# The first load of a streaming kernel as two transfers, of the even and of the odd partitions

## Chip, cores and metric

The kernel runs on one core of a Trainium2 chip. The metric is the device time of one execution in microseconds (us).

## The reference

```python
x = float32[32, 512, 2048]
x1, x2 = x[..., :1024], x[..., 1024:]
out = x1 * (1 / (1 + exp(-x1))) * x2          # silu(x1) * x2, float32[32, 512, 1024]
```

The kernel must read 134.2 MB and write 67.1 MB, and there is little arithmetic.

## The kernel before

The 16384 rows are taken in 16 tiles. In a tile each of the 128 partitions holds 8 whole rows (64 KB in, 32 KB out). Two input and two output buffers rotate. ScalarE issues the loads and does the silu, VectorE multiplies, and SyncE issues the stores. The first load is moved by hand ahead of the barrier that all engines pass at the start.

```python
def issue_ahead_of_the_first_barrier(nc):
    head, body = nc.main_func.blocks[:2]
    load = next(ins for ins in body.instructions if type(ins).__name__ == "InstDMACopy")
    ...                                     # cut: puts `load` before ScalarE's barrier drain

def load(i):
    xt = in_pool.tile([P, K, in_cols], dt, name="xt")              # K = 8, in_cols = 2048
    nc.scalar.dma_start(out=xt[:, :plan[i][1], :], in_=view(x_flat, i))
    loaded[i] = xt

load(0)
load(1)
for i in range(n_tiles):                                           # 16 tiles
    ...                                     # cut
    for c in range(0, k, KC):                                      # four chunks of two rows
        ...                                 # cut: silu into ot on ScalarE, then ot *= x2 on VectorE
        if last:
            nc.sync.dma_start(out=ov[:, c:ce, :], in_=ot[:, c:ce, :])
    if not last:
        nc.sync.dma_start(out=ov, in_=ot[:, :k, :])
    if i + 2 < n_tiles:
        load(i + 2)
```

Of the kernel before, what the change touches and what calls it, by code (L numbers as in the profile page):

```python
# [1 line left out]

# [4 lines left out]


def issue_ahead_of_the_first_barrier(nc):




    head, body = nc.main_func.blocks[:2]
    load = next(ins for ins in body.instructions if type(ins).__name__ == "InstDMACopy")
    at = next(
        j for j, ins in enumerate(head.instructions)
        if ins.engine == load.engine and type(ins).__name__ == "InstDrain"
    )
    body.instructions = [ins for ins in body.instructions if ins.name != load.name]  # L20
    head.instructions = head.instructions[:at] + [load] + head.instructions[at:]


@with_exitstack
def kernel(
    ctx: ExitStack,
    tc: tile.TileContext,
    x: bass.AP,
    out: bass.AP,
):  # L30






    nc = tc.nc
    P = nc.NUM_PARTITIONS

    x_flat = x.flatten_outer_dims()  # L40
    out_flat = out.flatten_outer_dims()
    num_rows, in_cols = x_flat.shape
    half = in_cols // 2
    dt = x_flat.dtype

    K = 8
    KC = 2
    PLAN = [K] * (num_rows // (P * K))

    in_pool = ctx.enter_context(tc.tile_pool(name="in_pool", bufs=2))  # L50
    out_pool = ctx.enter_context(tc.tile_pool(name="out_pool", bufs=2))

    plan = []
    row = 0
    for k in PLAN:
        plan.append((row, k))
        row += P * k
    assert row == num_rows
    n_tiles = len(plan)

    def view(flat, i):
        row0, k = plan[i]
        return flat[row0:row0 + P * k].rearrange("(p k) d -> p k d", k=k)

    nc.at_finalize(issue_ahead_of_the_first_barrier)


    ctx.enter_context(tc.manual_schedule())

    loaded = {}  # L70

    def load(i):
        xt = in_pool.tile([P, K, in_cols], dt, name="xt")
        nc.scalar.dma_start(out=xt[:, :plan[i][1], :], in_=view(x_flat, i))
        loaded[i] = xt

    load(0)
    load(1)
    for i in range(n_tiles):
        k = plan[i][1]  # L80
        xt = loaded.pop(i)
        last = i == n_tiles - 1
        ov = view(out_flat, i)
        ot = out_pool.tile([P, K, half], dt, name="ot")
        for c in range(0, k, KC):
            ce = min(c + KC, k)
            nc.scalar.activation(  # L87
                out=ot[:, c:ce, :],
                in_=xt[:, c:ce, :half],
                func=mybir.ActivationFunctionType.Silu,  # L90
            )
            nc.vector.tensor_mul(  # L92
                out=ot[:, c:ce, :],
                in0=ot[:, c:ce, :],
                in1=xt[:, c:ce, half:],
            )
            if last:
                nc.sync.dma_start(out=ov[:, c:ce, :], in_=ot[:, c:ce, :])
        if not last:
            nc.sync.dma_start(out=ov, in_=ot[:, :k, :])  # L100
        if i + 2 < n_tiles:
            load(i + 2)


# [1 line left out]
_INS = ['x']  # L106
_OUTS = [((32, 512, 1024), 'float32')]


# [23 lines left out]
```

## Time and profile before

| | before |
|---|---|
| time, median of 3 runs | 470.96 us (470.91 to 471.08) |
| span of the profiled run | 468.9 us |
| share of the 16 DMA engines' span that packets take | 66.4% loads + 33.2% stores |
| VectorE, ScalarE busy | 30%, 25% |

From the page of the kernel before: the DMA engines' busy tenths in 40 slices, the two queues (packets, MB, share of sixteen engines' span), the shares of the chain that ended last, and the activation table load (busy us, mean ns, idle time before it and what ended that).

```profile
span 468.9 us, 269 instructions
...
DMA  9899999999999998999999999999999989999998
...
q10 hardware_dynamic: 2304, 134.22, 66.4%
q1 hardware_dynamic: 2736, 67.11, 33.2%
...
DMA 80%; DVE 15%; ACT 3%; DVEq 0%; issue 0%
...
L87 ACT ACT_TABLE_LOAD x1 | 1.3, 1283 | 1.3 <-PEq L117 1.3
```

The two queue shares add to 99.6%: there is almost no moment at which a DMA engine has nothing to move. The chain alone would mislead here. It names loads, multiply and silu, because those steps hand the buffers round; but while the chain is in the multiply, the DMA still works on what was issued earlier (DMA share 0.95 and 412 GB/s from 46.48 to 55.39 us, the chain's first multiply).

The timeline of the kernel before, from its start to the first store (start us, duration us, engine, line, what; "x2" on an issue row merges two issues):

```profile
start us, us, engine line op out<-in xcount [idle before <-releaser]
0.13 1.13 ACTq L74 DMA_DIRECT2D xt<-in_x_dram  x2
...
1.29 1.28 ACT L87 ACT_TABLE_LOAD   x1 [1.29 <-PEq L117]
21.88 7.31 ACT L87 ACTIVATE ot<-xt 128x2048 f32<-128x2048 f32 x4 [19.31 <-DMA xt<-in_x_dram]
23.82 8.90 DVE L92 TENSOR_TENSOR ot<-ot,xt 128x2048 f32<-128x2048 f32 x4 [23.82 <-ACT ot L87]
32.74 0.38 SPq L100 DMA_DIRECT2D out_dram<-ot  x1
32.75 0.35 ACTq L74 DMA_DIRECT2D xt<-in_x_dram  x1
```

The first load is issued at 0.13 us and has landed at 21.88 us. The table that silu needs is loaded early, at 1.29 us, and costs nothing. The first store is issued at 32.74 us. The trace's single packet records add that the first packet starts at 1.14 us and that a 64 KB load packet takes 2.42 us on its engine.

### The profile page before, as it was taken

Reading aid. Unit: us, or ns where it says so; the run is one execution under the profiler, and the core shown is the slowest. Engines: PE = TensorE matmul, PEld = TensorE weight load, DVE = VectorE, ACT = ScalarE, POOL = GpSimd, SP = SyncE. Lnnn points to the kernel's source line nnn. Section 1 sums busy time; section 2 is a strip of 40 time slices with the busy share of each in tenths; the row PEclk is TensorE's granted clock in tenths of the full one; section 3 lists DMA queues with packets and bytes.
Section 4 is the critical chain, followed back from the end, with each engine's and each line's share of the span. In section 5 each row is a group of like instructions: output and inputs, shape, how many; then the busy total and the mean of one; then the engine's idle time right before and its main releaser. Section 6 shows DMA issues by size and latency. Waiting matters only on the chain.

```text
span 468.9 us, 269 instructions
## 1 busy us (share of the span) xinstructions
DVE 142.3 (30%) x64; ACT 118.2 (25%) x65; POOL 0.2 (0%) x4
## 2 busy tenths in 40 slices
DVE  0070705106061160601507025070250702407034
ACT  1142406023060330603206032060420604106051
POOL 0000000000000000000000000000000000000000
DMA  9899999999999998999999999999999989999998
GB/s 431 375 447 403 447 447 447 403 419 431 447 447 403 447 492 363 442 492 391 458 403 439 456 447 403 409 442 447 447 403 444 467 386 447 442 419 481 400 409 354
DMA packets 5042, 201.35 MB, mean 429 GB/s; under 512 B 560, under 2 KB 560, under 8 KB 560
## 3 DMA queue, kind: packets, MB, share of 16 engines
q10 hardware_dynamic: 2304, 134.22, 66.4%
q1 hardware_dynamic: 2736, 67.11, 33.2%
q14 instruction: 2, 0.02, 0.0%
HBM read 134.22 MB, written 67.11 MB: 429 GB/s over the span
## 4 chain that ended last, share of the span: by engine, by line
DMA 80%; DVE 15%; ACT 3%; DVEq 0%; issue 0%
DMA xt<-in_x_dram 80%; DVE ot L92 15%; ACT ot L87 3%; DVEq L128 0%
## 5 line engine op out<-in xcount | busy, mean ns | idle before, releaser
L92 DVE TENSOR_TENSOR ot<-ot,xt 128x2048 f32<-128x2048 f32 x64 | 142.3, 2286 | 319.5 <-ACT ot L87 319.5
L87 ACT ACTIVATE ot<-xt 128x2048 f32<-128x2048 f32 x64 | 116.9, 1897 | 338.8 <-DMA xt<-in_x_dram 338.8
L87 ACT ACT_TABLE_LOAD x1 | 1.3, 1283 | 1.3 <-PEq L117 1.3
L117 POOL MEMSET const-uint8-127<- 128x1 uint8 x1 | 0.1, 102 | 0.0
L117 POOL MEMSET const-bfloat16-1.0<- 128x1 bf16 x1 | 0.1, 101 | 0.0
L117 POOL MEMSET const-float32-0.0<- 128x1 f32 x1 | 0.1, 98 | 0.2 <-issue 0.2
L117 POOL MEMSET const-float32-1.0<- 128x1 f32 x1 | 0.1, 98 | 0.0
## 6 DMA issues: line engine op xcount, KB each, us to landing
out_dram<-ot SPq DMA_DIRECT2D x15, 4096.0 KB, 39.8
out_dram<-ot SPq DMA_DIRECT2D x4, 1024.0 KB, 5.7
xt<-in_x_dram ACTq DMA_DIRECT2D x16, 47.1
```

The lines of the kernel that those rows point to most:

```text
L87: nc.scalar.activation(out=ot[:, c:ce, :], in_=xt[:, c:ce, :half], func=mybir.ActivationFunctionType.Silu,)
L92: nc.vector.tensor_mul(out=ot[:, c:ce, :], in0=ot[:, c:ce, :], in1=xt[:, c:ce, half:],)
L117: nc = _bacc.Bacc("TRN2", target_bir_lowering=False, num_devices=1)
```

## The change

The intent is an earlier start: a first transfer of 64 partitions has half the packets (64 instead of 128; the trace has 2048 of 64 KB for 16 loads), so they might flow sooner. Both transfers stand ahead of the barrier. The split is by even and odd partitions, not by halves.

```diff
-def issue_ahead_of_the_first_barrier(nc):
+def issue_ahead_of_the_first_barrier(nc, count):
...                                   # cut: moves the first `count` loads instead of one
+    STARTING = [slice(0, None, 2), slice(1, None, 2)]
...
+    def load_parts(queue, dst, src, split):
+        for ps in STARTING if split else [slice(None)]:
+            queue.dma_start(out=dst[ps], in_=src[ps])
...
-        nc.scalar.dma_start(out=xt[:, :plan[i][1], :], in_=view(x_flat, i))
+        load_parts(nc.scalar, xt, view(x_flat, i), split=i == 0)
...
-            nc.sync.dma_start(out=ov, in_=ot[:, :k, :])
+            nc.sync.dma_start(out=ov, in_=ot)
```

The last line is the same access (k is always K).

More of the change, by code (lines that the diff above doesn't have):

```diff
@@ L6 @@
 from concourse._compat import with_exitstack
-def issue_ahead_of_the_first_barrier(nc):
+def issue_ahead_of_the_first_barrier(nc, count):
     head, body = nc.main_func.blocks[:2]
-    load = next(ins for ins in body.instructions if type(ins).__name__ == "InstDMACopy")
+    loads = [ins for ins in body.instructions if type(ins).__name__ == "InstDMACopy"][:count]
     at = next(
         j for j, ins in enumerate(head.instructions)
-        if ins.engine == load.engine and type(ins).__name__ == "InstDrain"
+        if ins.engine == loads[0].engine and type(ins).__name__ == "InstDrain"
     )
-    body.instructions = [ins for ins in body.instructions if ins.name != load.name]
-    head.instructions = head.instructions[:at] + [load] + head.instructions[at:]
+    names = {ins.name for ins in loads}
+    body.instructions = [ins for ins in body.instructions if ins.name not in names]
+    head.instructions = head.instructions[:at] + loads + head.instructions[at:]
 @with_exitstack
@@ L63, in view @@
         return flat[row0:row0 + P * k].rearrange("(p k) d -> p k d", k=k)
-    nc.at_finalize(issue_ahead_of_the_first_barrier)
+    nc.at_finalize(lambda nc: issue_ahead_of_the_first_barrier(nc, len(STARTING)))
     ctx.enter_context(tc.manual_schedule())
+    def load_parts(queue, dst, src, split):
+        for ps in STARTING if split else [slice(None)]:
+            queue.dma_start(out=dst[ps], in_=src[ps])
     loaded = {}
```

## The prediction

> **What bounds the kernel now.** The DMA engines. The page's DMA row reads 8 or 9 of 10 in all slices, at a mean of 429 GB/s; the two queues' packets take 66.4% + 33.2% = 99.6% of sixteen engines' span. VectorE is busy 30%, ScalarE 25%. The packets in the trace agree: from the first (1.14 us) to the last (467.63 us) about sixteen are in flight. A 64 KB load packet takes 2418 ns, a 32 KB store packet 1213 ns, an 8 KB one 309 ns; 2048, 1920 and 512 of them are 464.9 us on sixteen engines; the measured sum is 466.8 us. Most of the rest lies in two places: the first sixteen packets (about 3.0 instead of 2.42 us) and the sixteen before the first store (about 3.3 us). The chain of waits (80% loads, 15% multiply, 3% silu) is the loop that hands buffers back; the DMA never runs dry waiting for it.
>
> **What the change does.** (1) Load 0 (8.39 MB) becomes two transfers of 64 partitions each on one queue. Packet sizes and bytes stay: 4 + 4 instead of 8 packets per engine. (2) One more issue of about 0.35 us stands before ScalarE's barrier, so load 1 is issued at about 1.3 instead of 0.92 us, behind some 19 us of load 0: no cost. (3) The first tile waits for two semaphores. The instruction listing puts the second wait on the activation table load, so that load (1.28 us) moves from the idle time at 1.3 us to after the landing of tile 0. First silu, first store and load 2 come some 1.3 us later (store about 34.0 instead of 32.7 us). Load 1 still moves until past 40 us, so the DMA does not run dry: off the path. (4) The possible gain: the first packet starts 1.0 us after its issue. [...] first packets start an estimated 0 to 0.25 us earlier (half of the 0.38 us issue at most). Only this is on the critical path. (5) The full-tile store's slice is the same access.
>
> **Predicted time: 470.8 us, range 469.9 to 472.2.** Faster by over 2%: 1%; within 2%: 87%; slower by over 2%: 12%.
>
> **What would show it.** First packet at 0.9 to 1.15 us; landing of load 0 at 21.5 to 22.0 us; table load at about 21.8 us, first silu at about 23.1; DMA share and mean GB/s unchanged; last packet within 0.5 us of 467.6.
>
> **What would make it wrong.** [...] no trace here shows 64 strided ones. [...] load 0 runs at about half rate, packets near 4.8 us, landing near 41 us, an estimated +19 us (8 packets x 2.42 us): about 490 us. [...] Lesser risk: the later first store shifts the mixing of loads and stores; at most about 1 us.

The forecast comes to the 470.96 us before less about 0.2 us for the earlier start of step (4): 470.8. The condition of that gain, that the first packets of 64 rows come sooner than those of 128, was a supposition; the traced 0.38 us issue, of which half is 0.19, is all that the estimate has. Under "What would make it wrong" is an estimate: 4.8 us, 41 us and +19 us are what half of the traced rate (2.42 us per packet) comes to. It is no part of the 470.8 and lies outside the range, in the 12% for "slower by over 2%".

## More of the kernel before

All runs quoted here are at a granted clock of 1.0. Kernels sent together ran on one chip, beside the kernel before.

## The result, and the profile after

Ratios are computed as the mean time of one kernel's fast runs over that of the other's of the same rounds, so they are not quite the ratios of the medians.

| | before | after |
|---|---|---|
| time, median of 6 runs | 471.02 us (470.71 to 471.44) | 471.51 us (471.30 to 472.15) |
| ratio, 95% interval | | 1.0014 (1.0001 to 1.0027) |
| span of the profiled run | 468.9 us | 470.3 us |

The change is within 2%, and a little slower. The profiled run of the changed kernel took 472.13 us, near the top of its six, so its trace shows more than the typical loss.

The same lines of the page, of the changed kernel:

```profile
span 470.3 us, 272 instructions
...
DMA  9999999999999999999999999999999999999997
...
q10 hardware_dynamic: 2320, 134.22, 66.3%
q1 hardware_dynamic: 2736, 67.11, 33.1%
...
DMA 80%; DVE 15%; ACT 3%; DVEq 0%; issue 0%
...
L95 ACT ACT_TABLE_LOAD x1 | 1.3, 1283 | 22.4 <-DMA xt<-in_x_dram 22.4
```

Bytes, shares and chain are the same. The 16 new packets on the load queue are of 4 bytes: 272 with 17 transfers, 256 with 16. The trace has sixteen of them at 11.60 to 12.28 us, where the engines' fourth load packets end (11.60 to 12.29 us). One line differs: the table load now waits 22.4 us, for a load.

The timeline of the changed kernel:

```profile
0.13 2.20 ACTq L76 DMA_DIRECT2D xt<-in_x_dram  x3
...
22.36 1.28 ACT L95 ACT_TABLE_LOAD   x1 [22.36 <-DMA xt<-in_x_dram]
23.66 7.31 ACT L95 ACTIVATE ot<-xt 128x2048 f32<-128x2048 f32 x4
25.60 8.90 DVE L100 TENSOR_TENSOR ot<-ot,xt 128x2048 f32<-128x2048 f32 x4 [25.60 <-ACT ot L95]
34.52 0.38 SPq L108 DMA_DIRECT2D out_dram<-ot  x1
```

ScalarE sees the landing at 22.36 instead of 21.88 us (the last packet of load 0 ends 0.44 us later), the table load comes after it, and the first store is 1.78 us later. None of these lines says which of them costs time. For that the packets must be read.

**How the packets were read.** A record gives queue, start, duration and size, but not the engine. Each packet was therefore given to the engine whose previous packet ended at its start, which is a reconstruction: a second working of it, with other tolerances, moves single latenesses by up to 0.15 us. Three things were worked out for each run: the start of the first packet; when the engines' first store packets start (the earliest and the median of the first sixteen); and how late the slowest of the 16 engines is by 60 us (the end of its first packet, less 2.42 us, plus what its later load packets took beyond 2.42 us).

| | first packet | last engine ends its first packet | first store issued | first store packets, earliest / median | slowest engine late by | span |
|---|---|---|---|---|---|---|
| before | 1.14 | 4.60 | 32.74 | 38.9 / 39.1 | 3.04 | 468.87 |
| after | 1.45 | 5.04 | 34.52 | 39.2 / 42.2 | 4.89 | 470.35 |

Two things stand out. The first packet is 0.31 us later, not earlier: the first issue took 541 to 542 ns in two runs, against 376 ns before. That is 0.17 of the 0.31 us; the rest passes between the end of the issue and the first packet (0.78 instead of 0.64 us). And in the changed kernel the engines no longer begin to store together: two of them start 2.4 us or more ahead of the other 14 (39.2 and 39.7 against 42.1 to 42.7 us).

Followed to the end, these two are also the last to finish, at 468.87 and 469.03 us; the other 14 finish by 468.31. All 16 engines have 280 data packets in this reconstruction, and from 60 us on their load packets take the usual 2.42 us, so what is lost early stays lost. The last packet ends 1.41 us later than before. Of that, 0.30 is the later start and 0.06 the first packets, both as means over the 16 engines; 0.59 is the mean growth of the stalls at the first stores, and 0.46 is how much further the last engine lies behind the mean.

### The profile page after: what moved, and what is told of

It is laid out like the page before. It is cut to its first block, busy times and chain, and to the rows that moved or that the text cites. A ratio compares the mean times of both kernels' runs of the same rounds, so it can differ in the third digit from the quotient of the medians.

```text
span 470.3 us, 272 instructions
## 1 busy us (share of the span) xinstructions
DVE 142.4 (30%) x64; ACT 118.2 (25%) x65; POOL 0.2 (0%) x4
## 4 chain that ended last, share of the span: by engine, by line
DMA 80%; DVE 15%; ACT 3%; DVEq 0%; issue 0%
DMA xt<-in_x_dram 80%; DVE ot L100 15%; ACT ot L95 3%; DVEq L136 0%
## 5 line engine op out<-in xcount | busy, mean ns | idle before, releaser
L95 ACT ACT_TABLE_LOAD x1 | 1.3, 1283 | 22.4 <-DMA xt<-in_x_dram 22.4
```

Of the source, the lines that this page charges most:

```text
L95: nc.scalar.activation(out=ot[:, c:ce, :], in_=xt[:, c:ce, :half], func=mybir.ActivationFunctionType.Silu,)
```

## The experiments

Medians are of the kernel's own 4 to 6 runs against the kernel before on the same chip. In the edits, the lines that allocate `warm_pool` and `warm` are cut where they add nothing, and function names are shortened (`Silu` for `mybir.ActivationFunctionType.Silu`).

**The changed kernel again.** No edit.

> The changed kernel once more, to see how firm its +0.14% is. Start theory (the two 64-row issues bring the first packet 0.3 us later, and everything follows): first packet at 1.4 to 1.5 us, time +0.3 us (ratio 1.0006). Table theory (activation table load behind the landing makes the first store 1.3 us later, which lengthens the stall ahead of the first store): time +0.4 to +0.6 us, with the stalled packets ahead of the first store again over 3.4 us. Noise theory: ratio within 1.000 +- 0.0005.

Measured: 471.54 us against 470.90 (ratio 1.0016, interval 1.0003 to 1.0029). First packet at 1.45 us; one engine starts to store at 39.7 us, the median at 42.1. The loss came again, both intervals exclude 1, and noise is an unlikely cause. The trace of this run, the slowest of its five, shows one thing that the first does not: near the end the DMA engines run partly dry (last columns: DMA share, GB/s).

```profile
457.00:457.50 0.50, 0.50 (x2) 0.50 (x1) 0.00 (x0) 1.00 0.30 131
457.50:458.00 0.50, 0.50 (x1) 0.50 (x1) 0.00 (x0) 1.00 0.16 66
```

In the reconstruction twelve engines are idle there for 0.2 to 0.8 us: the first of them is done with the older store at 457.62 us, and the store of the last tile's first chunk, issued at 457.33, starts its first packet at 458.16. (In the first trace it is issued at 456.61, and nothing runs dry.) The end is still set by one engine, at 469.78 us; the other 15 finish by 468.35.

**Split, with the table loaded early.**

```diff
     load(0)
     load(1)
+    warm = warm_pool.tile([P, 2], dt, name="warm")
+    nc.vector.memset(warm[:, :1], 0.0)
+    nc.scalar.activation(out=warm[:, 1:], in_=warm[:, :1], func=Silu)
```

> The changed kernel with a one-column silu ahead, so that the table load is back at the start. First silu about 22.35 us instead of 23.66, first store about 33.2. Start theory: still +0.3 us against before, as the changed kernel. Table theory: back to before within 0.1 us, stall ahead of the first store about 0.8 us in each engine.

Measured: 471.37 us against 470.90 (1.0013, 1.0000 to 1.0025). First silu at 22.59 us, first store at 33.46. The time did not return to that of before, so an early table alone does not cure the loss. That the rest stays with the start is not shown: in this trace all engines begin to store within 0.9 us, and yet one ends at 469.12 us, 1.0 us after the other 15, for a reason that was not found. The stall ahead of the first store was about 1.05 us per engine, more than the 0.8 that the table theory asked for.

**One load, with a late table.**

```diff
     load(0)
     load(1)
+    nc.scalar.activation(out=warm, in_=loaded[0][:, 0, :1], func=Exp)   # meant to bring a second table load
```

> The kernel before, with a one-column exponential that waits for load 0 ahead of the first silu, so that the silu table is loaded only after the landing (about 1.3 to 1.6 us more until the first store, near 34.3). Start theory: time as before within 0.1 us. Table theory: +0.3 to +0.5 us, stall ahead of the first store over 1 us in each engine.

Measured: 471.79 us against 470.90 (1.0019, 1.0006 to 1.0031), with the first packet at 1.15 us and the first store at 34.41, 1.67 us later (one table load took 1.28 us in the kernels before and after). So +0.9 us with an unchanged start: the start cannot be all. This looks like the table theory, but the delay of the store and the table load itself are not yet told apart.

**One load, behind the barrier.**

```diff
-    nc.at_finalize(issue_ahead_of_the_first_barrier)
```

> The kernel before with load 0 issued after the barrier: a measure of what a later first packet is worth. First issue at about 0.6 to 0.9 us instead of 0.13, so the first packet 0.5 to 0.75 us later. Start theory: the time grows by that much (+0.5 to +0.75 us, ratio about 1.0013), one for one. If the start is not what counts: within 0.2 us of before.

Measured: 471.82 us against 470.90 (1.0017, 1.0003 to 1.0030); first packet at 1.75 us, 0.61 later. The time grew by 0.9 us, more than the 0.5 to 0.75 expected; the interval reaches from 0.1 to 1.4 us, so it agrees with a late start that is paid in full, and does not fix the rate.

**The kernel before, against itself.** No edit.

> The kernel before, against itself: how far two sets of runs of one program lie apart, and a second trace of it. Ratio 1.000 within 0.0005; first packet at 1.14 us; stall ahead of the first store again about 0.87 us per engine (sixteen packets of about 3.3 us).

Measured: 470.98 us against 471.17 (0.9996, 0.9983 to 1.0009), first packet at 1.15 us, sixteen stalled packets, slowest engine 3.17 us late. Two sets of runs of one program differ by 0.2 us in the median. Single executions stray further: one of the 11 of the kernel before took 472.5 us, and one of the six with the 2.4 us delay 472.64.

**One load, first tile delayed by scratch work: 0.8, 2.4 and 4.0 us.** The three differ in the columns only:

```diff
     load(0)
     load(1)
+    nc.scalar.activation(out=warm[:, :850], in_=loaded[0][:, 0, :850], func=Silu)
...                             # the other two: two such lines, of 2048 and 300, of 2048 and 1900 columns
```

> The kernel before, with one extra silu of 850 columns into a scratch tile ahead of the first tile: first store about 0.8 us later (33.5 us), table load and first packet unchanged. Start theory: time as before. Later-is-worse theory (a later first store costs in proportion): about +0.4 us. Phase theory (what counts is where the first store falls in the 2.42 us that one load packet takes): between 0 and +0.6 us.

> The same with about 2.3 to 2.5 us of scratch silu: the first store one whole load packet later (about 35.2 us). Start theory: as before. Later-is-worse theory: +1.0 us or more, as the 1.67 us delay of the late table cost +0.9. Phase theory: back to before within 0.2 us, stall ahead of the first store about 0.87 us per engine.

> The same with about 3.9 us of scratch silu: first store near 36.7 us, one load packet after that of the late-table run (34.4). Start theory: as before. Later-is-worse theory: +2 us. Phase theory: about +0.9 us as the late-table run, with engines that switch to stores one packet apart.

Measured, first store at 33.72, 35.19 and 36.44 us: 470.83, 471.09 and 471.10 us against 471.17 (0.9992, 0.9999, 0.9994; all intervals hold 1). A first store up to 3.7 us later costs nothing that these times can see, and "later is worse" falls. (The traces of the two longer delays are 0.3 and 0.4 us longer than that of the kernel before, again, which the times don't resolve.) The phase theory, as it was put, missed too: it expected +0.9 us at the longest delay. That run came out at 36.44 us rather than one whole packet after the late-table run (which would be 36.83), so it did not test the intended phase. In the two longer delays the engines still begin to store together, within 0.8 us. In the shortest they do not: 13 begin at 39.0 to 39.6 us and three at 41.9 to 42.1. No engine there loses more than 1.4 us to stalls, and the last packet ends at 467.71 us, as before (467.62). So engines out of step need not be costly.

This led to the straggler theory, a reading of these traces that the next runs test. The end of the program is set by the slowest of 16 equally loaded DMA engines (280 data packets each; in the changed kernel the two that were ahead end last, at 468.87 and 469.03 us). If one or two engines take their first store packet a packet ahead of the others, they stall twice where the others stall once, and nothing afterwards lets them catch up.

**One load, delayed by 1.5 us**, to the moment of the late-table run, with no second table load (the same edit with 1670 columns).

> The kernel before, with about 1.5 us of scratch silu ahead of the first tile, so that the first store is issued near 34.4 us, as in the late-table run, but with no second table load. Straggler theory (when the first store is issued about 0.5 to 1.2 us after the engines' last packet starts, one or two engines pick it up a packet ahead of the rest and stall twice; the slowest engine sets the end): first store packets spread over more than 2 us, the slowest engine over 4.3 us late by 60 us, time +0.5 to +0.9 us. Table theory (the table load itself costs): as before, within 0.2 us, as the delays of 1.0, 2.5 and 3.7 us were.

Measured: 471.68 us against 470.93 (1.0012, 1.0000 to 1.0025). The timeline shows the first store at 34.31 us:

```profile
21.95 1.60 ACT L81 ACTIVATE warm<-xt 128x1670 f32<-128x1670 f32 x1 [19.37 <-DMA xt<-in_x_dram]
...
34.31 0.37 SPq L103 DMA_DIRECT2D out_dram<-ot  x1
```

The earliest store packet starts at 39.2 us, the median at 41.9, and the slowest engine is 4.95 us late. Three engines of the reconstruction, from 35.6 us on (L is a load packet, S a store packet; start + duration in us):

```
this run, an ordinary engine   L 35.64+2.42 | L 38.05+3.90 | S 41.95+1.21 | S 43.16+1.21 | L 44.37+2.42
this run, the engine ahead     L 35.89+3.34 | S 39.22+1.21 | L 40.43+4.36 | S 44.79+1.21 | S 46.01+1.21
kernel before, one engine      L 35.71+3.24 | S 38.95+1.21 | L 40.16+2.42 | S 42.58+1.21 | S 43.79+1.21
```

The engine ahead loses 0.92 us at its first stall, as all engines do in the kernel before (0.8 to 1.0 us). Then it loses another 1.94 us while the rest stall; the ordinary engine loses 1.48 us once. In the four runs with one or two engines ahead, these engines lose 2.3 to 2.9 us in all, and no other engine more than 1.7. In the late-table run, too, the engine ahead ends last, at 468.86 us, with the other 15 done by 467.86. The delays of 0.98, 2.45 and 3.70 us cost nothing that shows in the times, and this one between them does, so neither lateness nor the table load is needed for the loss. Two of the five executions took 471.1 us, as the kernel before; the profiled one is the slowest, so an engine ahead is shown for that one only.

**Split, delayed by 1.1 us more**, so that the first store meets the engines at the point of their packets where the kernel before meets them (the same edit with 1190 columns, on the changed kernel).

> The changed kernel with 1.1 us of scratch silu more, so that its first store (near 35.65 us) falls 1.6 to 2.3 us after the engines' packet starts, as in the kernel before. Straggler theory: first store packets within 1 us of each other, the slowest engine 3.5 to 4.0 us late, time +0.3 to +0.45 us against before, which is faster than the changed kernel's +0.65. Later-is-worse: slower than the changed kernel.

Measured: 471.20 us (471.18 to 471.42) against 470.93 (1.0006, 0.9993 to 1.0018). It does more work on the first tile than the changed kernel, stores later (35.67 us), and is closer to the kernel before. First store packets are at 41.7 / 42.1 us, and the slowest engine is 3.96 us late. The remaining +0.27 us is about the 0.31 us by which its first packet is late, though its own interval holds 1. The interval overlaps that of the changed kernel, which ran on another chip, so the times alone do not prove the step; the trace shows no engine ahead.

**Split by halves.**

```diff
-    STARTING = [slice(0, None, 2), slice(1, None, 2)]
+    STARTING = [slice(0, 64), slice(64, 128)]
```

> The changed kernel, split at partition 64 instead of by even and odd. [...] load 0 packets near 4.8 us, landing near 41 us, time about +19 us (490 us). If the engines' own rate is all that limits: as the changed kernel. The first issue's duration tells whether the 541 ns come from the 64 rows (again about 541) or from the step of two (about 375).

Measured: 491.31 us against 470.93 (1.0431, 1.0416 to 1.0445). Bandwidth while only loads run (last columns: DMA share, GB/s), first of the changed kernel, then of the halves:

```profile
core 0: us, DVE busy (x) ACT busy (x) POOL busy (x), PEclk, DMA share, GB/s
5.00:20.00 15.00, 0.00 (x0) 0.00 (x0) 0.00 (x0) 1.00 1.00 433
```

```profile
5.00:20.00 15.00, 0.00 (x0) 0.00 (x0) 0.00 (x0) 1.00 1.02 210
```

All 16 engines are busy in both (shares 1.00 and 1.02), but in the halves each packet takes 5.12 us instead of 2.42. The runs don't show why; they show that 64 partitions in a row ran at about half the rate (210 GB/s), and 64 in steps of two did not (433). The clause cut from the expectation gave a ground that no trace shows; what is left of that estimate is again half of the traced rate. The first issue took 548 ns, as for the even partitions (541), so its length comes with the 64-row transfer, not with the step of two.

**Two transfers of all 128 partitions**, each with half of every partition's rows.

```diff
-    STARTING = [slice(0, None, 2), slice(1, None, 2)]
+    STARTING = [slice(0, K // 2), slice(K // 2, K)]
...
-            queue.dma_start(out=dst[ps], in_=src[ps])
+            queue.dma_start(out=dst[:, ps], in_=src[:, ps])
```

> Load 0 in two transfers ahead of the barrier, but of all 128 partitions, each with half of every partition's rows (32 KB a packet). If it is the 64-row transfer that starts late: first issue about 375 ns, first packet at 1.14 us as before; if it is two issues in a row, near 1.45 us. The first tile's work begins after half the load (first silu near 12 us), first store near 28.5 us. Time within 0.3 us of before if no engine is split from the rest; +0.5 to +0.9 if one is.

Measured: 471.97 us against 470.93 (1.0022, 1.0009 to 1.0036). The first issue took 376 ns and the first packet starts at 1.14 us, as before: two issues in a row did not delay the start here, 64-row transfers did (first issue 541 to 548 ns; first packet at 1.45 us in the changed kernel). No engine is ahead of the others (34.2 / 34.3 us). The expectation of a time within 0.3 us failed, and for another reason. Two windows near the end, of this run:

```profile
455.00:457.00 2.00, 1.56 (x1) 2.00 (x2) 0.00 (x0) 1.00 0.91 393
457.00:458.50 1.50, 1.50 (x2) 1.50 (x2) 0.00 (x0) 1.00 0.01 0
```

and of the kernel before:

```profile
455.00:457.00 2.00, 2.00 (x2) 2.00 (x2) 0.00 (x0) 1.00 0.68 295
457.00:458.50 1.50, 1.50 (x2) 1.34 (x1) 0.00 (x0) 1.00 0.96 404
```

Windows count a packet where it starts, so single shares are rough, but 0.01 means that no data packet starts for 1.5 us; from the packets' ends each DMA engine is idle for 0.7 to 1.6 us. The earlier first store (28.38 us) shifted the turns of loads and stores. The last load landed at 453.5 instead of 451.0 us, and the store before the last tile's had drained in 15 of 16 engines by 457.6 us, before the last tile's first chunk was ready (issued at 457.76). In the kernel before that chunk is issued at 455.29 us and the first engine is done with the older store at 457.0, a margin of 1.7 us. In the two traces of the changed kernel this margin is 1.2 and 0.3 us; in the second the engines ran partly dry, as said above.

**The runs together** (us; "late" is the slowest engine at 60 us; the last two experiments, with other packets or idle engines, are left out):

| run | first packet | first store packets, earliest / median | late | span | span − late | median minus before |
|---|---|---|---|---|---|---|
| before, again | 1.15 | 39.0 / 39.2 | 3.17 | 468.95 | 465.8 | −0.2 |
| delay 2.4 | 1.15 | 41.6 / 41.9 | 3.71 | 469.27 | 465.6 | −0.1 |
| delay 4.0 | 1.14 | 41.9 / 42.0 | 3.69 | 469.38 | 465.7 | −0.1 |
| split, delay 1.1 | 1.45 | 41.7 / 42.1 | 3.96 | 469.42 | 465.5 | +0.3 |
| split, early table | 1.46 | 39.4 / 39.6 | 4.11 | 470.45 | 466.3 | +0.5 |
| behind the barrier | 1.75 | 39.7 / 39.9 | 4.03 | 469.95 | 465.9 | +0.9 |
| late table | 1.15 | 39.2 / 42.0 | 4.73 | 470.13 | 465.4 | +0.9 |
| delay 1.5 | 1.13 | 39.2 / 41.9 | 4.95 | 470.33 | 465.4 | +0.8 |
| changed | 1.45 | 39.2 / 42.2 | 4.89 | 470.35 | 465.5 | +0.5 |
| changed, again | 1.45 | 39.7 / 42.1 | 5.20 | 471.12 | 465.9 | +0.6 |

(The delay of 0.8 us belongs here too, with first store packets at 39.0 / 39.2 us, three of them near 42, and a slowest engine about 3.4 us late.) Spans differ by 2.2 us, but the span less the lateness of the slowest engine stays within 465.4 to 466.3. That is most of the differences and not all: the early table has the second longest span with an ordinary lateness. The four runs with a gap of over 2 us between earliest and median store packet are the four with the latest engines.

## Why the prediction was right, and where its steps failed

- **The bound, and the size: right.** The time is inside the range and within 2%. Sixteen DMA engines that are busy for 99.6% of the span leave only the two ends and single stalls to change. The sign was not right: 470.8 us forecast a gain of 0.2 us, and a loss of 0.5 came. It fell inside the range because the range left room for the "lesser risk".
- **The half rate: the risk was real, but not for this split.** The even and odd transfers ran at 2.42 us per packet. The halves ran at 5.12, and cost 20.4 us where the prediction gave an estimate of 19 for a half-rate load.
- **The start (step 4): wrong in direction.** It expected the first packet 0 to 0.25 us earlier; it came 0.31 us later (1.45 instead of 1.14), of which 0.17 us is the issue of a 64-row transfer (541 ns instead of 376) and the rest a longer time from the issue's end to the first packet. The halves show the same issue with contiguous rows (548 ns), and two 128-row transfers do not show it (376 ns, 1.14 us). The landing (22.36 as ScalarE sees it, instead of 21.5 to 22.0), the issue of load 1 (1.99 instead of 1.3, as the second issue took 604 ns) and the silu (23.66 instead of 23.1) are later in the same sense.
- **The table load (step 3): right, but not the whole.** It moved behind the landing as the instruction listing had it, and a later store alone cost nothing in three delays (ratios 0.9992, 0.9999 and 0.9994). What the prediction missed: the moment of the first store also bears on whether the engines switch to stores together. With it at 32.74 and 35.19 us they did, at 34.31 and 34.41 they did not (earliest 39.2, median 41.9 and 42.0). In the two traces of the changed kernel they did not either (39.2 and 42.2, 39.7 and 42.1), so the first store was not "off the path". The "lesser risk", a shifted mixing of loads and stores at about 1 us at most (estimate, with no number behind it), names the right place, not the mechanism.
- **The last packet within 0.5 us of 467.6: wrong in the trace,** which has 469.0. Of the 1.4 us, some 0.4 us is the later start and first packets, and most of the rest the longer stalls at the first stores, twice over in the two engines that end last.

So the +0.5 to +0.6 us has two parts. The later start alone leaves about +0.3 us (split, delay 1.1; its interval holds 0). An engine ahead of the others alone goes with +0.8 us (delay 1.5) in a kernel with an unchanged start. The engines that run partly dry near the end, in one of the two traces, are not the one that sets its end. Whether every unprofiled run of the changed kernel has a split engine can't be seen; its times, from 471.25 to 472.89 us, suggest that they differ.

What stays open is why an engine stalls by about a packet's third when the first stores arrive (0.8 to 1.0 us of 2.42 in the kernel before), and what exactly decides which engine is ahead. In the four split runs the first store was issued 0.5 to 1.2 us after the engines' latest packet starts; in the kernel before 1.6 to 2.0, in the longest delay 0.2 to 0.7. The delay of 0.8 us, where three engines fell behind, has 0.1 to 0.6 in 13 engines and 2.3 to 2.4 in three. That is a description of these runs, not a rule. Open, too, is where the lone late engine of the early-table run comes from, and the single executions above 472 us of kernels whose trace has no engine ahead.

No version tried beats the kernel before: the best ratio, 0.9992 for the delay of 0.8 us, is inside the noise of the kernel against itself (0.9996).

## What to carry to other kernels

Here 16 equally loaded DMA engines (280 data packets each) were busy for over 99% of the span, and the end was the slowest engine's end (469.03 us in the changed kernel, with 14 engines done by 468.31). In such a kernel look at single packets for engines that fall out of step, and don't trust a mean share. Splitting a first transfer by partitions did not start it sooner here: it issued more slowly (541 ns instead of 376, first packet at 1.45 us instead of 1.14), and it hung the table load onto a wait for data (22.4 us instead of 1.3), which the instruction listing showed beforehand. A later event off the critical path was not free of effect here: a first store 1.57 us later went with +0.8 us, while 0.98, 2.45 and 3.70 us later cost nothing visible. So test it by delaying it by several amounts, not one.
